# A hybrid retention and attention block: values made token-major, and the last 16 tokens on their own in float32

## The chip, the cores and the metric

The kernel runs on one core of a Trainium2 chip. The core has five engines that run side by side, each with its own queue of instructions: PE (TensorE, matrix multiplies), DVE (VectorE), ACT (ScalarE), POOL (GpSimd) and SP (SyncE, here only the weights' transfers). PE writes its results into PSUM, a small memory of eight banks a partition; everything else lies in SBUF or in the chip's DRAM. The metric is the device time of one execution in microseconds, lower is better.

## The reference

One transformer block, in float32, over 512 tokens with 16 learned "meta" tokens put ahead of them (528 in all), width 1024: a half-weight SwiGLU feed-forward, a mixer, and a second feed-forward. The change touches the mixer.

```python
def hybrid_mixer(u, pos, k_top, w_in, w_ret_out, w_att_out, w_mix_out):
    proj = u @ w_in                       # u: 528 x 1024, normalised
    rq, rk, rv, rg, aq, ak, av, iq, ik, iw, g_ret, g_att = jnp.split(proj, offs, axis=-1)
    rq, rk = rope(rq), rope(rk) * RET_DK ** -0.5          # 4 heads, 256 wide
    yr = retention(rq, rk, rv)                            # values: 4 heads, 512 wide
    yr = (jax.nn.silu(rg) * yr) @ w_ret_out
    ya = dsa_attention(rope(aq), rope(ak), av, rope(iq), rope(ik), iw, k_top) @ w_att_out   # 8 heads, 128 wide
    return (jax.nn.sigmoid(g_ret) * yr + jax.nn.sigmoid(g_att) * ya) @ w_mix_out
```

`retention` weighs the values of each head with decaying scores of query and key. `dsa_attention` picks for each query its 128 best keys by an index score and does a softmax over those and the meta tokens. Both need, for each head, a sum over the tokens of score times value.

## The kernel before, in words

**Layout.** Activations lie feature-major: 128 features on the partitions, the 528 tokens along the free axis; the normalised input is eight such tiles (`xs(0)` to `xs(7)`, KD = 8). Every operand of PE is split into a high and a low part (`split`: ACT copies to the rounded type float32r, DVE subtracts), and a product is three matmuls: high x high, low x high, high x low (`mm3`, L145). A weight tile of 128 columns is loaded by SP's queue (`load_w`; `raw`, two buffers of 1 MB), split (`split_w`, three buffers) and used for 8 x 3 matmuls. Over all 528 tokens a matmul is cut into two of 264 columns (`proj_all`, `halves`), over the 512 tokens whose outputs are kept it has 512 (`proj_real`).

**Order.** The order on PE is that of the code, written out by hand (`manual_schedule`). The other engines' order comes from a planner that goes by priority, program order and the buffers that are free. PSUM in the mixer is two tiles of two banks (`mm_tile`) and four of one bank (`sm_tile`). A buffer is given out again when the last reader of its tile is done.

**Index part** (L568 to 604): four blocks of index queries into the four one-bank tiles (`psiq`), then index keys (`psik`) into the next that comes free; rotary embedding (`rope_swap`) on ACT, POOL and DVE. The scores themselves (`index_steps`) and the selection of keys (`select_steps`) are generators, of which `step()` runs a bit between pieces of other work. The index scores' matmuls (L620) have 64 rows and go in pairs onto the two halves of the array's rows.

**Retention heads** (L803 to 877), for each of four heads: two blocks of queries, two of keys, the output projection of the head before (`last_out`), then for each of four blocks of 128 value columns: the values (`values`, L854: projection into `psrv` over 528 tokens, times the norm R on DVE), the gate (`gated`), and `by_token` (L788): five transposes on PE (L791, L792) that turn the 128 x 528 block into token-major pieces, split into `vh`, `vl` and a small tail tile for the last 16 tokens. `weigh` (L777) then multiplies them with the scores: 12 matmuls and one for the tail (L775), whose three 16-row parts stand at rows 0, 32 and 64 of `vtail`.

**Attention heads** (L974 to 992), for each of eight heads: scores, query and key projections of the next head, transposes of the probabilities (`transpose_p`), the value projection of the next head (`proj_v`, `psav`), the weighing, and `by_token`. In the last head four gates (`gate`, `psgate`) stand where the next head's projections would be; the two other gates of this kind and the eight of the other (`psga`) come after, in the pool `ou`.

Of the kernel before, what the change touches and what calls it, by code (L numbers as in the profile page):

```python
# [81 lines left out]
def kernel(ctx: ExitStack, tc: tile.TileContext, x, meta, g1, wg1, wu1, wd1, gm,  # L82
# [117 lines left out]
    def rstd_steps(ssum, n, dim, dst, sp, psum):  # L200


        ends = [min(b * P, n - P) for b in range(-(-n // P))]
        nb = len(ends)
        col = psum()
        for b, t0 in enumerate(ends):
            nc.tensor.matmul(col[:, b : b + 1], ssum[:, t0 : t0 + P], ones, start=True, stop=True)
        yield from rstd_of(col, n, dim, dst, sp, psum, P - (n - S))

    def rstd_of(col, n, dim, dst, sp, psum, tail):  # L210
# [4 lines left out]
        r = sp.tile([P, 5], F32, tag="rcol", name="rcol", bufs=2)  # L215
# [34 lines left out]
    hd = dpool.tile([KD, P, S], F32, name="hd")  # L250

# [4 lines left out]
    gap(cpool, 8)  # L256


    with pool("f1") as fp, pool("gps", 2, PSUM) as gps, ExitStack() as later:
# [205 lines left out]
        for f0, nf in ((0, 12), (12, 10)):  # L465
# [38 lines left out]
            for c in range(0, KD, 2):  # L504
# [7 lines left out]
                for i in range(2):  # L512
                    k = c + i
                    nc.vector.scalar_tensor_tensor(hT[k], halves(pss[i])[1], 0.5, hT[k], ALU.mult, ALU.add)
                    if f0:
                        h, l = new_x(k, XO)
                        split_gain(hT[k], gains[:, 1, k : k + 1], h, l)
                        add_square(hT[k], ssum2, k == 0, fp, bufs=4)
                        nc.scalar.dma_start(hd[k], hT[k][:, REAL])
# [48 lines left out]
    with pool("ixt") as ixt:  # L568
        tp.update(pool=ixt, bufs=8)
        norm = rstd_steps(ssum2, T, D, R2, ixt, lambda: mm_tile("psn"))  # L570
        pss = []
        cols = Cols(w_in, OFF_IQ, 4)
        for i in range(4):
            w = cols.next()
            ps = sm_tile("psiq")[:, :NL]
            mm3([(ps, LATE)], w, xs, KD)
            pss.append(ps)
            if i < 3:
                next(norm)
        cos, sin = rope_tables(0, ixt)  # L580
# [8 lines left out]
        ps = sm_tile("psik")  # L589
# [60 lines left out]
    def tails(p, n):  # L650

        tp.update(v=[stacked(p, f"vtail{i}", P) for i in range(2)], p=stacked(p, "ptail", n), turn=0)
# [27 lines left out]
    with pool("rt") as rt:  # L680
        tp.update(pool=rt, bufs=7)
        cos, sin = rope_tables(2, rt)
# [85 lines left out]
        def weighted(ps, vb, prob):  # L768

            for kb in range(4):  # L770
                vh, vl = vb[0][:, kb, :], vb[1][:, kb, :]
# [3 lines left out]
            nc.tensor.matmul(ps[:, KQ[4] :], vb[2][:TR], tp["p"][:TR, :NM], start=False, stop=True)  # L775

        def weigh(c, vb, sg, prob, ssum, o):  # L777
# [5 lines left out]
            oh = rt.tile([P, S], F32R, tag=f"oh{c}", name="oh")  # L783
            ol = rt.tile([P, S], F32R, tag=f"ol{c}", name="ol")
            split(t[:, :S], oh, ol)
            o.append((oh, ol))

        def by_token(vt, vp):  # L788
            ps = mm_tile("psvt").rearrange("p (a b) -> p a b", a=2)
            for kb in range(4):  # L790
                nc.tensor.transpose(ps[:, 0, kb * P : (kb + 1) * P], vt[:, kb * P : (kb + 1) * P], ident)  # L791
            nc.tensor.transpose(ps[:NM, 1, 0:P], vt[:, 4 * P : T], ident)  # L792
            vh = vp.tile([P, 4, P], F32R, tag="vh", name="vh", bufs=2)
            vl = vp.tile([P, 4, P], F32R, tag="vl", name="vl", bufs=2)
            split(ps[:, 0, :].rearrange("p (b c) -> p b c", b=4), vh, vl)
            tail = tp["v"][tp["turn"]]
            tp["turn"] ^= 1
            split_rows(ps[:NM, 1, 0:P], tail, "hhl")
            return vh, vl, tail
# [3 lines left out]
        for h in range(RH + 1):  # L803
            if h == RH:
# [4 lines left out]
                break  # L809
            u = rt.tile([P, UW], F32, tag="u", name="u")  # L810
            nc.scalar.dma_start(u, decay[h])
            cols = Cols(w_in, OFF_RQ + h * DK, 2)
            if h == 0:
                steps, bg[0] = bg[0], iter(())
# [9 lines left out]
            cols = Cols(w_in, OFF_RK + h * DK, 2)  # L824
            if h == 0:
                bg[0] = steps
            ka = proj_all(cols, "psrk")
            next(norm, None)
            step()
            kb_ = proj_all(cols, "psrk")  # L830
            next(norm, None)
            rk = rope_pair(ka, kb_, cos, sin, T, "rk")
            step()
# [8 lines left out]
            cv = Cols(w_in, OFF_RV + h * DV, 4)  # L842
# [11 lines left out]
            def values():  # L854
                ps = proj_all(cv, "psrv")
                vt = tmp()
                ins = nc.vector.tensor_tensor(vt, ps, R, ALU.mult)
                step(ins)
                return vt

            for c in range(4):
                if c == 0:
                    sg = gated()
                    vt = values()
                    prob = decayed(rq, rk, u)
                else:
                    vt = values()
                    sg = gated()
                    weigh(*pend, prob, ssum, o)
                if h == 0:  # L870
                    step()
                    step()
                pend = (c, by_token(vt, rt), sg)
# [9 lines left out]

    with pool("ao") as ao:
        ao_parts = []
        with pool("at") as at:
# [11 lines left out]
            cq, ck, cv = (Cols(w_in, o_, AH, step=1) for o_ in (OFF_AQ, OFF_AK, OFF_AV))  # L898
# [20 lines left out]
            def proj_v():  # L919
                w = cv.next()  # L920
                parts, ps = halves(mm_tile("psav"))
                mm3(parts, w, xs, KD)
                vt = tmp()
                nc.vector.tensor_tensor(vt, ps, R, ALU.mult)
                return vt
# [40 lines left out]
            def weigh_v(parts, v):  # L966
                ps = sm_tile("psao")
                weighted(ps, v, parts)
                oh = ao.tile([P, S], F32R, tag=f"ah{len(ao_parts)}", name="ah")
                ol = ao.tile([P, S], F32R, tag=f"al{len(ao_parts)}", name="al")  # L970
                split(ps, oh, ol)
                ao_parts.append((oh, ol))

            q, k, vt = proj_q(), proj_k(), proj_v()  # L974
            for h in range(AH):
                more = h + 1 < AH
                scores(q, k)
                if h == 0:
                    v = by_token(vt, at)
                if more:  # L980
                    q, k = proj_q(), proj_k()
                else:
                    for c in (2, 3, 4):
                        gate_acc(c, gate(gr, at, wide=True))
                parts = transpose_p()
                if more:
                    vt = proj_v()
                else:
                    gate_acc(5, gate(gr, at, wide=True))
                weigh_v(parts, v)  # L990
                if more:
                    v = by_token(vt, at)
# [5 lines left out]
        with pool("ou") as ou:  # L998
            tp.update(pool=ou, bufs=3)
            for c in (6, 7):  # L1000
                gate_acc(c, gate(gr, ou))
            cols = Cols(w_in, OFF_GA, KD)
            sa = []
            for c in range(KD):
                w = cols.next()
                ps = sm_tile("psga")
                mm3([(ps, REAL)], w, xs, KD)
                t = ou.tile([P, S], F32, tag=f"sa{c}", name="sa")
                nc.vector.tensor_tensor(t, ps, Rr, ALU.mult)
                nc.scalar.activation(t, t, AF.Sigmoid)  # L1010
                sa.append(t)
# [54 lines left out]
    mgs.close()  # L1066
    accs.close()
# [117 lines left out]
```

## Time and profile before

| | |
|---|---|
| runs before, us | 1591.03, 1591.54, 1591.64 (median 1591.54) |
| profiled execution | 1590.52 us, span 1588.7 us |
| granted TensorE clock | 0.999 |
| PE busy | 1576.4 us, 99% of the span |
| DVE, ACT, POOL busy | 820.0, 569.3, 230.9 us |
| retention heads, about | 422 to 868 us of the span |
| attention heads, about | 868 to 1076 us |

Rows name line, engine, operation, output<-inputs, shape, count, busy time and mean duration. PE's matmuls overlap: one with 512 columns is shown as 389 ns long, but the next starts 227 ns after it. So starts and stretches are read for PE, not durations. In the timeline and the chain the first two numbers of a row are start and length in us.

### The profile page before, as it was taken

The page shows a single profiled execution, that of the slowest core. Times are in us where ns is not written, and L with a number is a line of the kernel's source. Part 1 is how long each engine was busy: PE and PEld are TensorE (multiplying, and loading weights), DVE is VectorE, ACT ScalarE, POOL GpSimd, SP SyncE. Part 2 cuts the span into 40 slices and gives each one's busy share as a digit, 9 for nine tenths or more (in the row PEclk, how much of TensorE's full clock was granted, in tenths as well). Part 3 has the DMA queues.
Part 4 walks back from the last instruction along what each step waited for, and adds up shares of the span by engine and source line. Part 5 has one row for each costly group of instructions (what it writes and reads, how often), then busy time and mean ns, then how long its engine had stood idle before and what let it go on. Part 6 is the DMA issues. An engine that isn't in the chain of part 4 may idle for free.

```text
span 1588.7 us, 23011 instructions
## 1 busy us (share of the span) xinstructions
PE 1576.4 (99%) x9731; PEld 1419.7 (89%) x9731; DVE 820.0 (52%) x1263; ACT 569.3 (36%) x912; POOL 230.9 (15%) x187
## 2 busy tenths in 40 slices
PE   9999999999999999999999999999999999999998
PEld 8999999999888898899898999988888888888886
DVE  5443234334575776866845766753454444334434
ACT  6322222223544333233333555552234332223223
POOL 1211001111310201302204110011002111001100
PEclk9999999999999999999999999999999999999999
DMA  5222232224422231231313322322233332232222
GB/s 192 83 89 78 97 109 80 97 80 141 134 88 67 67 116 54 80 117 40 120 54 92 95 67 67 93 72 88 91 128 108 111 105 81 94 113 86 93 92 81
DMA packets 148582, 148.66 MB, mean 94 GB/s; under 512 B 3288, under 2 KB 137456, under 8 KB 148480
## 3 DMA queue, kind: packets, MB, share of 16 engines
q1 hardware_dynamic: 143872, 138.16, 27.0%
q10 hardware_dynamic: 4544, 9.03, 1.7%
q8 instruction: 76, 1.25, 0.3%
q14 instruction: 26, 0.21, 0.0%
q0 software_dynamic: 64, 0.01, 0.0%
HBM read 143.00 MB, written 4.19 MB: 93 GB/s over the span
## 4 chain that ended last, share of the span: by engine, by line
PE 94%; DVE 3%; ACT 1%; issue 1%; POOL 1%; DMA 0%; ACTq 0%; POOLq 0%; DVEq 0%
PE psu L152 16%; PE psg L152 15%; PE psd L152 8%; PE psd L1146 7%; PE psrv L152 6%; PE psrg L152 6%; PE psrk L152 3%; PE psak L152 3%; PE psav L152 3%; PE psrq L152 3%; PE psgate L152 3%; PE psro L152 3%; PE psmo L152 3%; PE psaq L152 3%; PE psat L152 3%; PE psga L152 3%
## 5 line engine op out<-in xcount | busy, mean ns | idle before, releaser
L117 ACT ACTIVATE whi<-raw 128x1024 fp32r<-128x1024 f32 (+3 forms) x284 | 278.0, 981 | 840.1 <-PE psu L152 165.5
L118 DVE TENSOR_TENSOR wlo<-raw,whi 128x1024 fp32r<-128x1024 f32 (+3 forms) x284 | 339.7, 1196 | 177.2 <-ACT whi L117 173.6
L152 PE MATMUL psu<-xl,whi 128*128 128x264 f32 (+1 forms) x528 | 141.0, 319 | 0.0
L152 PE MATMUL psu<-xh,whi 128*128 128x264 f32 (+1 forms) x528 | 140.6, 318 | 0.0
L152 PE MATMUL psu<-xh,wlo 128*128 128x264 f32 (+1 forms) x528 | 140.5, 318 | 0.0
L152 PE MATMUL psg<-xl,whi 128*128 128x264 f32 (+1 forms) x496 | 133.3, 321 | 0.0
L152 PE MATMUL psg<-xh,whi 128*128 128x264 f32 (+1 forms) x496 | 132.8, 320 | 0.0
L152 PE MATMUL psg<-xh,wlo 128*128 128x264 f32 (+1 forms) x496 | 132.8, 321 | 0.0
L152 PEld LDWEIGHTS psu<-xh,wlo 128*128 128x128 f32 x528 | 88.1, 188 | 6.8
L152 PEld LDWEIGHTS psu<-xh,whi 128*128 128x128 f32 x528 | 87.8, 188 | 6.9
L152 PEld LDWEIGHTS psu<-xl,whi 128*128 128x128 f32 x528 | 87.5, 188 | 6.9
L152 PEld LDWEIGHTS psg<-xh,wlo 128*128 128x128 f32 x496 | 82.6, 188 | 6.8
L152 PEld LDWEIGHTS psg<-xh,whi 128*128 128x128 f32 x496 | 82.3, 188 | 6.8
L152 PEld LDWEIGHTS psg<-xl,whi 128*128 128x128 f32 x496 | 82.0, 188 | 6.8
L486 POOL TENSOR_TENSOR t<-t,R 128x528 f32<-128x528 f32 x22 | 37.6, 1711 | 262.3 <-ACT t L485 262.3
L1121 POOL TENSOR_TENSOR t<-t,R 128x512 f32<-128x512 f32 x22 | 38.5, 1751 | 251.6 <-ACT t L1120 251.6
L152 PE MATMUL psd<-hl,whi 128*128 128x264 f32 x352 | 71.3, 284 | 0.0
L152 PE MATMUL psd<-hh,wlo 128*128 128x264 f32 x352 | 70.8, 283 | 0.0
L152 PE MATMUL psd<-hh,whi 128*128 128x264 f32 x352 | 70.6, 282 | 0.0
L1146 PE MATMUL psd<-whi,hh 128*128 128x512 f32 x176 | 68.5, 389 | 0.0
L1146 PE MATMUL psd<-wlo,hh 128*128 128x512 f32 x176 | 68.5, 389 | 0.0
L1146 PE MATMUL psd<-whi,hl 128*128 128x512 f32 x176 | 68.5, 389 | 0.0
(316 smaller groups left out, 3543.1 us busy)
## 6 DMA issues: line engine op xcount, KB each, us to landing
raw<-in_w_in_dram SPq DMA_DIRECT2D x34, 1024.0 KB, 4.9
raw<-in_ffn_w_up_dram SPq DMA_DIRECT2D x22, 1024.0 KB, 5.0
raw<-in_ffn_w_gate_dram SPq DMA_DIRECT2D x21, 1024.0 KB, 5.0
raw<-in_w_in_dram SPq DMA_DIRECT2D x25, 512.0 KB, 3.4
raw<-in_ffn_w_down_dram SPq DMA_DIRECT2D x10, 1024.0 KB, 4.8
raw<-in_w_ret_out_dram SPq DMA_DIRECT2D x16, 512.0 KB, 3.4
raw<-in_ffn_w_down_dram SPq DMA_DIRECT2D x8, 768.0 KB, 4.3
raw<-in_ffn_w_down_dram SPq DMA_DIRECT2D x8, 640.0 KB, 3.9
```

Source lines behind the costliest of these rows:

```text
L117: nc.scalar.activation(hi, src, AF.Copy)
L118: eng.tensor_tensor(lo, src, hi.bitcast(F32), ALU.subtract)
L152: nc.tensor.matmul(o, a[:, k, :], b[:, sl], start=first and k == 0 and i == 0, stop=last and k == nk - 1 and i == 2)
L486: nc.gpsimd.tensor_tensor(t, t, R, ALU.mult)
L1121: nc.gpsimd.tensor_tensor(t, t, R, ALU.mult)
L1146: nc.tensor.matmul(pss[b], a[:, bs], m[:, k % 2, :], start=k0 + k == 0 and i == 0, stop=k0 + k == nf - 1 and i == 2)
```

## The change

1. **Values token-major.** `values` takes a head's 512 value columns at once (for attention: four heads at once, twice). The token blocks are now the stationary operand and 512 columns of weights the moving one, by pairs of row blocks of the weights. Four results (`psv`, 128 tokens x 512 columns each) fill both two-bank tiles. They come out token-major, so `by_token` and its transposes go. The norm is applied in the split (`split_gain` with a column of `rtok`), into one high and one low tile `vo`; `weigh` later writes its output over the values that it has used.
2. **The last 16 tokens.** Their part is done in float32, unsplit, from the raw weights: `xlast` holds those 16 columns of the normalised input, padded to 32, for each row block, and 32 matmuls a group write the four 128-column blocks into four groups of 32 partitions of one tile (`psvl`). It is done in two stretches of 16, after the first and the third pair of row blocks.
3. **Their parts through DRAM.** The result is split, both parts are written to a DRAM tile `vd`, and three DMAs bring them to rows 0, 32 and 64 of `vtail`, which is now one tile 512 wide. All five are on POOL's queue.
4. **Gates inside the heads.** Where `proj_v` stood in attention heads 0, 1, 2, 4, 5 and 6 there is now one retention gate each; head 3 has the second half of the values there. The last head has three attention gates. Five of those stay in `ou`.
5. **Order.** In head 0 the keys come ahead of the queries, and index steps run from the start. The scores (`decayed`) come behind all values. `psik` and `psao` take two-bank tiles.

```diff
@@ end of feed-forward 1, for each feature block k
+                        nc.gpsimd.tensor_scalar(xlast[:, k, :NM], hT[k][:, S:], gains[:, 1, k : k + 1], None, ALU.mult)
@@ index part
+        nc.gpsimd.tensor_tensor(xlast[:, :, :NM], xlast[:, :, :NM], R[:, S:].unsqueeze(1).to_broadcast([P, KD, NM]), ALU.mult)
-        ps = sm_tile("psik")
+        ps = mm_tile("psik")[:, :S]
@@ new
+    def values(c0, parts, vp, meanwhile=lambda: None):
+        two = [mm_tile("psv") for _ in range(2)]
+        ps = [two[b // 2][:, b % 2 * S : (b % 2 + 1) * S] for b in range(4)]
+        rest = sm_tile("psvl")[:, :P]
+        for k0 in range(0, KD, 2):
+            if k0 % 4 == 0:
+                raw = wpool.tile([P, 2048], F32, tag="raw", name="raw", bufs=2).rearrange("p (k c) -> p k c", k=4)
+                for i in (0, 2):
+                    rows = slice((k0 + i) * P, (k0 + i + 2) * P)
+                    nc.sync.dma_start(raw[:, i : i + 2], w_in[rows, c0 : c0 + 4 * P].rearrange("(k p) c -> p k c", p=P))
+            wh, wl = split_w(raw[:, k0 % 4 : k0 % 4 + 2, :])
+            for b in range(4):
+                bs = slice(b * P, (b + 1) * P)
+                for k in range(2):
+                    xh, xl = xs(k0 + k)
+                    for i, (a, m) in enumerate(((xh, wh), (xl, wh), (xh, wl))):
+                        nc.tensor.matmul(ps[b], a[:, bs], m[:, k, :], start=k0 + k == 0 and i == 0,
+                                         stop=k0 + k == KD - 1 and i == 2)
+                if k0 == KD - 2:
+                    split_gain(ps[b].rearrange("p (c d) -> p c d", c=4), rtok[:, b : b + 1],
+                               parts[0][:, :, bs], parts[1][:, :, bs])
+                if b % 2:
+                    meanwhile()
+            if k0 % 4 == 0:
+                for k in range(k0, k0 + 4):
+                    for c in range(4):
+                        nc.tensor.matmul(rest[32 * c : 32 * c + 32], xlast[:, k, :], raw[:, k % 4, c * P : (c + 1) * P],
+                                         start=k == 0, stop=k == KD - 1)
+                if k0:
+                    rh, rl = (vp.tile([P, P], F32R, tag=f"rest{i}", name="rest") for i in range(2))
+                    split(rest, rh, rl)
+                    for i, part in enumerate((rh, rl)):
+                        nc.gpsimd.dma_start(vd[i], part.bitcast(F32))
+                    for r, i in ((0, 0), (32, 0), (64, 1)):
+                        nc.gpsimd.dma_start(tp["v"][r : r + NM].bitcast(F32).rearrange("q (c d) -> q c d", c=4),
+                                            vd[i].rearrange("(c q) d -> q c d", q=32)[:NM])
+        return [(parts[0][:, c, :], parts[1][:, c, :], tp["v"][:TR, c * P : (c + 1) * P]) for c in range(4)]
@@ retention head
+            if h == 0:
+                rk = rope_pair(*keys(), cos, sin, T, "rk")
             cols = Cols(w_in, OFF_RQ + h * DK, 2)
...
+            vs = values(OFF_RV + h * DV, parts, rt, step)
+            prob = decayed(rq, rk, u)
...
             for c in range(4):
+                sg = gated()
+                if c:
                     weigh(*pend, prob, ssum, o)
...
-                pend = (c, by_token(vt, rt), sg)
+                pend = (c, vs[c], sg)
@@ attention heads
-            q, k, vt = proj_q(), proj_k(), proj_v()
+            q, k = proj_q(), proj_k()
+            vs = half_values(0)
             for h in range(AH):
                 more = h + 1 < AH
                 scores(q, k)
-                if h == 0:
-                    v = by_token(vt, at)
                 if more:
                     q, k = proj_q(), proj_k()
                 else:
-                    for c in (2, 3, 4):
-                        gate_acc(c, gate(gr, at, wide=True))
-                parts = transpose_p()
-                if more:
-                    vt = proj_v()
+                    wide_gate_a()
+                    wide_gate_a()
+                pt = transpose_p()
+                if h == 3:
+                    more_vs = half_values(1)
+                elif more:
+                    wide_gate()
                 else:
-                    gate_acc(5, gate(gr, at, wide=True))
-                weigh_v(parts, v)
-                if more:
-                    v = by_token(vt, at)
+                    wide_gate_a()
+                weigh_v(h, pt, vs[h])
+                if h == 3:
+                    vs += more_vs
```

## The prediction

> **What bounds the kernel now.** I read the page first: the busy shares, then the chain that ended last, by engine.
>
> ```profile
> span 1588.7 us, 23011 instructions
> PE 1576.4 (99%) x9731; PEld 1419.7 (89%) x9731; DVE 820.0 (52%) x1263; ACT 569.3 (36%) x912; POOL 230.9 (15%) x187
> PE 94%; DVE 3%; ACT 1%; issue 1%; POOL 1%; DMA 0%; ACTq 0%; POOLq 0%; DVEq 0%
> ```
>
> TensorE is busy for all but 12 us of the span, so the question is only how much PE time the change takes out, how much it puts in, and whether a new wait opens. Next come the view of waits with PE as the waiting engine (us in total, times, longest) and the table of windows, for the heads (retention head 1, then all of the attention).
>
> ```profile
> PE psik L152 <- DVE tmp L552: 1.2, 1, 1.2
> PE psrg L152 <- DVE wlo L118: 0.9, 2, 0.6
> PE psst L754 <- DVE tmp L758: 0.5, 1, 0.5
> PE psrq L152 <- ACT tmp L623: 0.5, 1, 0.5
> ...
> 540.00:646.00 106.00, 106.00 (x646) 95.27 (x645) 79.00 (x142) 35.04 (x58) 10.14 (x9) 1.00 0.26 84
> 868.00:1076.00 208.00, 207.95 (x1436) 194.59 (x1435) 139.53 (x314) 113.19 (x227) 33.87 (x32) 1.00 0.28 83
> ```
>
> PE waits for almost nothing, and in both stretches it is busy from end to end, while DVE (79 of 106, 140 of 208 us) and ACT have room. So every microsecond of PE work counts in full, and the gates that move into the attention heads are worth nothing by themselves: they are as many matmuls as before, and there are no holes there for them to fill.
>
> **The profiled execution.** It took 1590.52 us, its span 1588.7 and 1.8 around it, which is 1.0 below the median of 1591.54. I make the sum as a difference and add it to the median.
>
> **Removed: the transposes.** The tile view counts them, the timeline shows one set.
>
> ```profile
> L791 PE MATMUL psvt<-ident,tmp x96: 271/273/329, 463.6 to 1047.7; 128*128 128x128 f32 x96
> L792 PE MATMUL psvt<-ident,tmp x24: 272/273/273, 464.1 to 1047.9; 128*16 128x128 f32 x24
> ...
> 590.58 0.17 PE L775 MATMUL pspv<-ptail,vtail 80*128 80x16 f32 x1
> 590.61 0.65 PE L791 MATMUL psvt<-ident,tmp 128*128 128x128 f32 x4
> 591.09 0.27 PE L792 MATMUL psvt<-ident,tmp 128*16 128x128 f32 x1
> 591.12 0.49 PE L152 MATMUL psrv<-xh,whi 128*128 128x264 f32 x2
> ```
>
> Durations on PE overlap, so starts are what counts. From the first transpose to the first matmul behind the set, 590.61 to 591.12, are 0.51 us. There are 24 sets: 24 x 0.51 = -12.2 us. The two DVE and three ACT instructions of a set, and the multiply by R, go too; they lay beside PE and are worth nothing here.
>
> **Changed: the values' own matmuls.** The chain in order of time gives pure streams (start, us, count).
>
> ```profile
> 577.53 5.78 PE psrv L152 x48
> ...
> 590.76 0.50 PE psvt L791 x4
> 591.26 0.11 PE psvt L792
> 591.37 5.77 PE psrv L152 x48
> ...
> 1353.19 65.28 PE psd L1146 x288
> ```
>
> Before, a group of four 128-column blocks takes 4 x 48 matmuls with 264 columns, 4 x 5.77 = 23.08 us. Afterwards it is 4 row blocks x 8 x 3 = 96 matmuls with 512 columns, tokens stationary and weights moving. L1146 has that form: 65.28 / 288 = 0.227 us each, so 21.76 us. The gain is 1.32 us a group; four retention heads and two attention halves make 6 groups: -7.9 us.
>
> **Added: the last 16 tokens in float32.** That is 8 x 4 = 32 matmuls a group, 192 in all, each with 32 stationary columns and 128 moving ones, on one of four column groups of the array. No such matmul is in the trace, so I bound it. First, what is a float32 matmul there? L207 issues five of them for this norm, and the rows show ten loads and ten matmuls.
>
> ```profile
> 400.74 1.19 PEld L207 LDWEIGHTS psn<-ones,ssum 128*128 128x128 f32 x10 [0.20 <-POOL ssum L245]
> 400.75 1.28 PE L207 MATMUL psn<-ones,ssum 128*128 128x1 f32 x10
> ```
>
> So each becomes two records with a weight load each. How long is a record with 128 float32 columns? The nearest row is the float32 transpose above: 0.11 us from one to the next. So 64 records of 0.11 a group. Can those on different column groups overlap? The nearest rows are the index scores, pairs of matmuls on two row halves of the array.
>
> ```profile
> 451.14 0.39 PE L152 MATMUL psrg<-xh,wlo 128*128 128x512 f32 x1
> 451.46 0.50 PE L620 MATMUL pssc<-ikh,iqh 64*128 64x512 f32 x2
> 451.80 0.40 PE L620 MATMUL pssc<-ikl,iqh 64*128 64x512 f32 x2
> 452.03 0.39 PE L620 MATMUL pssc<-ikh,iql 64*128 64x512 f32 x2
> 452.36 0.51 PE L152 MATMUL psrv<-xh,whi 128*128 128x264 f32 x2
> 452.70 0.28 PE L152 MATMUL psrv<-xl,whi 128*128 128x264 f32 x1
> ```
>
> Two matmuls of 512 columns on different halves together take the 0.23 us of one (451.80 to 452.03), and the next on the same half starts only after that. I carry this over to column groups: different groups overlap, one group doesn't overlap itself. But the two records of one float32 matmul are on one group, and they are neighbours in the queue. If starts keep the queue's order, as all rows here do, the second waits for the first (0.11), the next group's first starts with it, and so on: one record's time for each matmul, not a quarter of it. 32 x 0.11 = 3.5 us a group.
>
> Getting into and out of such a stretch costs too. Entering takes 0.32 us (451.14 to 451.46) against the usual 0.227, the first pair 0.34 against 0.23, leaving 0.33 against 0.23, the first two matmuls behind it 0.34 against the 2 x 0.12 of the stream: about 0.4 in all. The code goes into it twice a group (after row blocks 0 and 1, and 4 and 5): 12 x 0.4 = +4.8.
>
> The ends for 192 such matmuls: all four groups side by side, 16 x 0.11 x 6 = 10.6; no overlap, 64 x 0.11 x 6 = 42.2. The middle is 21.1, and I take it, because the row pairs have this very behaviour. With the switching: +25.9 us.
>
> The Trainium skill (TensorE: Matmul & The Clock Gate, Part 3, Measured speedup vs the span model) counts tiles of the array as starting about 4 ns apart, so that four cost little more than one. By that alone the stretch would have the lower end's 10.6. For row halves the trace agrees (a pair inside one matmul's time), for column groups no run here shows it yet.
>
> **Moved: the keys ahead of the queries in head 0, and psik into a two-bank tile.** There are two such tiles. psik takes the one that the second key projection needs next.
>
> ```profile
> 414.81 0.33 PE L152 MATMUL psiq<-xl,whi 128*128 128x384 f32 x1
> 414.98 0.34 PE L152 MATMUL psiq<-xh,wlo 128*128 128x384 f32 x1
> 416.54 0.47 PE L152 MATMUL psik<-xh,whi 128*128 128x512 f32 x1 [1.22 <-DVE tmp L552]
> ...
> 426.56 1.22 DVE L118 TENSOR_TENSOR wlo<-raw,whi 128x1024 fp32r<-128x1024 f32 x1
> ...
> L592 ACT ACTIVATE tmp<-psik x1: 591/591/591, 428.2 to 428.2; 32x512 f32<-32x512 f32 x1
> L593 ACT ACTIVATE tmp<-psik x1: 590/590/590, 428.8 to 428.8; 32x512 f32<-32x512 f32 x1
> L594 DVE TENSOR_TENSOR tmp<-psik,cos x1: 682/682/682, 429.4 to 429.4; 64x512 f32<-64x512 f32 x1
> L596 DVE TENSOR_TENSOR iw<-psik,R x1: 684/684/684, 430.1 to 430.1; 8x512 f32<-8x512 f32 x1
> ```
>
> psik no longer waits for a bank (416.54 instead of one step of 0.17 after 414.98: -1.4). It then ends near 420.6 (24 x 0.227), the first key block 5.77 later, at 426.4. The second needs psik read out, and the last reader ends at 430.8 behind the ropes of the index queries; the next weights are split only at 427.8. So a new wait of 1.4 to 4.4 us opens; since the readers stand behind the same ropes as before, I take +3.0. Behind the waiting matmul stand the queries of head 0, whose readers wait along. The one multiply of xlast by R on POOL ahead of the tables is inside these bounds.
>
> **Added: the way through DRAM.** Five DMAs a group on POOL's queue: two out, three back. Rows for such transfers, with us to landing, and one issue on POOL:
>
> ```profile
> hd<-hT ACTq DMA_DIRECT2D x8, 256.0 KB, 2.1
> hc<-hd ACTq DMA_DIRECT2D x8, 256.0 KB, 2.6
> grow<-in_mix_norm_dram POOLq DMA_DIRECT2D x1, 4.0 KB, 4.8
> ...
> L277 POOL DMA_DIRECT2D grow<-in_mix_norm_dram x1 | 0.7, 748 | 0.0
> ```
>
> Splits 0.6, two issues 1.4, landing 2.1 to 4.8, one more issue 0.7, landing 2.6 to 4.8: 7.4 to 12.3 us. In the retention heads the reader (L775) comes after the last quarter of the values, the scores and two gates, some 20 us later, and POOL's adds and ropes behind the DMAs aren't due earlier: nothing. The cover is gone in one place. In attention head 3 the second half's values come ahead of weigh_v, and its last matmul reads the same tail tile, which that half has just asked to have rewritten. Its cover is 24 x 0.227 = 5.4 and the 12 matmuls of the weighing, about 2.0. So PE waits 0 to 4.9 us there; I take +2.0, nearer to the rows that go through a DRAM tile. Loads on SP are as many bytes in somewhat more issues, and the other three waits of PE stay: 0.
>
> **The sum.** -12.2 - 7.9 + 25.9 - 1.4 + 3.0 + 2.0 = +9.4 us: 1591.5 + 9.4 = 1601 us.
>
> **Rivals.**
> A: all four column groups run side by side, or a record is half as long (the float32 row that I used is a transpose). Then 10.6 instead of 21.1: -1.1, 1590; with the two new waits at their lower ends (1.4 and 0) -4.7, 1587, which is faster. For it speaks that a pair of row halves costs no more than one matmul, against it the order of the two records. It decides for faster from about 8 us less than my sum up to that end. Chance 0.32. (The rule of the Trainium skill named above would give this case.)
> B: column groups don't overlap at all. +21.1 more: 1622. Against it speak the pairs of row halves; for it, that no row shows columns. Chance 0.15.
> C: DVE becomes the bound, with values' splits and the selection in one stretch. Against it: 79 of 106 us in head 1, and DVE loses work. It would add a few us at most; 0.03, inside the range.
>
> **How the numbers follow.** The forecast's case has 0.5, with its own range of 1594 to 1607 (the waits at their ends, the switching between 0 and its price). Case A reaches from 1585 to 1592, B stands at 1622. A range from 1585 to 1611 leaves out B and a little. Within 0.2% is 1588.4 to 1594.7, about what a measurement can tell. Of A some 0.22 is faster, 0.1 inside; of the forecast 0.03 inside. So faster 0.22, same 0.13, slower 0.65.
>
> **What would show it.** L791 and L792 gone; psv at 0.227 us a matmul; the stretch of 16 float32 matmuls (32 records) about 1.8 us long between its neighbours, against 0.9 in A and 3.5 in B; PE waiting at the second psrk of head 0, and at L775 of attention head 3. Wrong would make me above all the length of that stretch.

## The result, and the profile after

The changed kernel took 1614.42 us (median of 4 runs, 1613.54 to 1616.76) where the kernel before, on the same chip, took 1591.59 (1591.03 to 1591.93): a ratio of 1.0146, 95% interval 1.0129 to 1.0164. It is 22.8 us slower. The forecast was 1601, slower by 9.4, in a range up to 1611: the sign was right, the size was not, and the time lies outside the range. The sign is luck: it comes from a wait that the forecast did not have, and without that wait the terms measured below come out about even. The profiled execution of the changed kernel is its 1613.54 run, with a span of 1611.8 us at a granted clock of 0.998; beside the 1588.7 of before that is 23.1 us, and the sums below are made against these 23.1.

First the page, the span and the busy times, the chain by engine, and one group of instructions:

```profile
span 1611.8 us, 22507 instructions
PE 1575.1 (98%) x9419; PEld 1385.3 (86%) x9419; DVE 803.5 (50%) x1221; ACT 574.9 (36%) x882; POOL 254.5 (16%) x224
...
PE 91%; DVE 3%; ACT 2%; issue 1%; DMA 1%; POOL 1%; ACTq 0%; POOLq 0%; DVEq 0%
...
L683 PE MATMUL psv<-whi,xh 128*128 128x512 f32 x192 | 78.2, 407 | 20.2 <-DVE vo L122 18.9
```

TensorE is busy for 1.3 us less than before, in a span that is 23 us longer. So the loss is not work that PE was given; PE waits. The last row already says where: the matmuls of the values (psv) stood idle for 20.2 us, 18.9 of them until DVE had written vo, the values' low part. The view of waits, PE as the waiting engine (us in total, times, longest), gives the list:

```profile
PE psv L683 <- DVE vo L122: 18.9, 12, 1.7
PE psrk L152 <- DVE iw L605: 3.4, 1, 3.4
...
PE psrq L152 <- ACT wt L619: 1.4, 1, 1.4
PE psv L683 <- DVE tmp L560: 1.3, 1, 1.3
PE psS L980 <- DVE vo L122: 1.0, 1, 1.0
```

Twelve waits of one kind: two in each of the six groups of values. The chain of the changed kernel, in order of time, shows a group's two (start, us, what):

```profile
587.12 1.01 PE psvl L693 x32
588.13 1.60 PE psv L683 x6
...
589.75 0.70 ACT vo L121
...
590.47 0.76 DVE vo L122
...
591.28 3.05 PE psv L683 x12
...
594.35 0.70 ACT vo L121
...
595.07 0.76 DVE vo L122
...
595.88 1.66 PE psv L683 x6
```

The timeline of PE, of the same kernel, around the first of them (start, us, operation, and in brackets the idle time ahead and what ended it):

```profile
586.73 0.39 PE L683 MATMUL psv<-wlo,xh 128*128 128x512 f32 x1
587.05 1.08 PE L693 MATMUL psvl<-raw,xlast 128*32 128x128 f32 x32
588.06 0.50 PE L683 MATMUL psv<-whi,xh 128*128 128x512 f32 x1
588.40 0.40 PE L683 MATMUL psv<-whi,xl 128*128 128x512 f32 x1
...
589.33 0.39 PE L683 MATMUL psv<-wlo,xh 128*128 128x512 f32 x1
591.28 0.50 PE L683 MATMUL psv<-whi,xh 128*128 128x512 f32 x1 [1.56 <-DVE vo L122]
591.61 0.40 PE L683 MATMUL psv<-whi,xl 128*128 128x512 f32 x1
```

This is the last pair of row blocks of a group. Six matmuls finish token block 0; ACT splits off its high part (0.70), DVE its low part (0.76); and only then do the matmuls of token block 1 begin, which have nothing to do with block 0's values. The chain goes PE, ACT, DVE, PE in turn. It happens for blocks 0 to 1 and 2 to 3, and not for 1 to 2. Blocks 0 and 1 lie in one two-bank tile of PSUM, blocks 2 and 3 in the other (`two[b // 2][:, b % 2 * S : ...]`). That the tile as a whole is what a write waits for is tested below.

The second reading is the stretch of float32 matmuls. The tile view of psvl (duration in ns min/median/max, first and last start, shape) counts its records:

```profile
L693 PEld LDWEIGHTS psvl<-raw,xlast x384: 106/110/110, 457.1 to 1024.3; 128*32 128x32 f32 x192
L693 PE MATMUL psvl<-raw,xlast x384: 272/273/298, 457.1 to 1024.4; 128*32 128x128 f32 x192
```

192 matmuls are 384 records, two each. A stretch of 16 (32 records) begins at 587.05, and the next psv at 588.06: 1.01 us, where the forecast said about 1.8, rival A 0.9, rival B 3.5. With both edges, from the start of the last psv ahead (586.73) to that of the second behind (588.40), it takes 1.67, less two ordinary steps of 0.227: 1.22 us a stretch, 14.6 for twelve.

One thing about the changed kernel is no matter of time. In attention head 3 `half_values(1)` stands ahead of `weigh_v`, and both halves keep the last 16 tokens in the one tile `vtail`. The timelines of POOL and of PE have the last transfer into it ahead of the matmul that reads it:

```profile
1031.93 0.51 POOL L701 DMA_DIRECT2D vtail<-vd  x1 [1.08 <-DMA vd<-rest]
1035.85 0.17 PE L828 MATMUL psao<-ptail,vtail 80*128 80x16 f32 x1
```

So the code weighs the last 16 tokens of head 3 with the values of head 7, in the changed kernel and in e1 to e4, e7 and e11 below. The matmuls and transfers are as many either way. In e8 to e10 the second half comes behind that weighing, and each head reads its own values.

### The profile page after: what moved, and what is told of

Its sections match the earlier page's. It is cut to its first block, busy times and chain, and to the rows that moved or that the text cites. A ratio compares the mean times of both kernels' runs of the same rounds, so it can differ in the third digit from the quotient of the medians.

```text
span 1611.8 us, 22507 instructions
## 1 busy us (share of the span) xinstructions
PE 1575.1 (98%) x9419; PEld 1385.3 (86%) x9419; DVE 803.5 (50%) x1221; ACT 574.9 (36%) x882; POOL 254.5 (16%) x224
## 3 DMA queue, kind: packets, MB, share of 16 engines
q8 instruction: 74, 1.21, 0.3%
## 4 chain that ended last, share of the span: by engine, by line
PE 91%; DVE 3%; ACT 2%; issue 1%; DMA 1%; POOL 1%; ACTq 0%; POOLq 0%; DVEq 0%
PE psu L152 15%; PE psg L152 15%; PE psv L683 8%; PE psd L152 8%; PE psd L1182 7%; PE psrg L152 6%; PE psro L152 4%; PE psgate L152 3%; PE psmo L152 3%; PE psga L152 3%; PE psat L152 3%; PE psaq L152 3%; PE psak L152 3%; PE psrq L152 2%; PE psrk L152 2%; PE pspv L827 2%
## 5 line engine op out<-in xcount | busy, mean ns | idle before, releaser
L683 PE MATMUL psv<-whi,xh 128*128 128x512 f32 x192 | 78.2, 407 | 20.2 <-DVE vo L122 18.9
L152 PE MATMUL psro<-vo,whi 128*128 128x512 f32 x256 | 79.1, 390 | 0.0
L683 PE MATMUL psv<-wlo,xh 128*128 128x512 f32 x192 | 75.0, 391 | 0.6 <-DVE wlo L118 0.6
L683 PE MATMUL psv<-whi,xl 128*128 128x512 f32 x192 | 75.0, 390 | 0.0
```

Of the source, the lines that this page charges most:

```text
L152: nc.tensor.matmul(o, a[:, k, :], b[:, sl], start=first and k == 0 and i == 0, stop=last and k == nk - 1 and i == 2)
L683: nc.tensor.matmul(ps[b], a[:, bs], m[:, k, :], start=k0 + k == 0 and i == 0, stop=k0 + k == KD - 1 and i == 2)
```

## The experiments

Ratios are to the kernel before, run on the same chip each time. The first four stand beside the changed kernel; most later ones build on the first.

**e1_split_late: both splits after both blocks of a tile.** If psv waits because a two-bank tile is one thing to those who write it, the waits go with this; the work stays the same.

```
-                if k0 == KD - 2:
-                    split_gain(ps[b] ..., bs)
                 if b % 2:
+                    if k0 == KD - 2:
+                        for d in (b - 1, b):
+                            split_gain(ps[d] ..., ds)
                     meanwhile()
```

> The splits of a pair of token blocks are issued after both blocks' matmuls. Theory 1 (the wait of PE on DVE in the last quarter of the values, 18.9 us in 12 waits, is there because two results share one two-bank tile: the readers of the first half hold back the writes to the second): the 12 waits go, with the 0.11 us of start-up behind each, about -20 us against the changed kernel, 1594 us. Rival (ACT and DVE are simply behind there, and the wait comes back at the next thing that needs them): -5 us at most, 1609 us or more, with new waits at the scores and gates of about the same sum.

Measured: 1595.58 us, ratio 1.0031 (1.0021 to 1.0041), span 1594.6. The same work in another order takes 17.2 us less span than the changed kernel. In the view of waits psv's for vo are gone, and what stays is small:

```profile
PE psrk L152 <- DVE iw L605: 4.4, 1, 4.4
PE psv L683 <- DVE tmp L560: 2.0, 1, 2.0
...
PE psS L982 <- DVE vo L118: 1.4, 1, 1.4
```

How much were the twelve waits worth? From the starts of PE, a group of a retention head is 3.73 us shorter here than in the changed kernel, in each of the four heads (27.98 against 24.24 in head 1). I take the same for the two groups of the attention, whose other waits differ between the kernels (the second one takes 28.07 in the changed kernel, 3.83 above 24.24): 22.4 for six. That is more than the 18.9 of the view, since idle time is counted from a matmul's end, and its row (0.39) is longer than its step (0.227), and since the first step after a wait is 0.1 longer (591.28 to 591.61). Some of it came back as the last rows above: PE reaches other places sooner than ACT and DVE do.

Some came back as clock. The table of windows (us; busy PE, PEld, DVE, ACT, POOL; granted clock, DMA share, GB/s) gives the four us behind the wait for iw, of e1 and then of the changed kernel:

```profile
431.00:435.00 4.00, 3.88 (x19) 3.91 (x20) 2.87 (x4) 2.32 (x3) 0.62 (x3) 0.57 0.67 201
431.00:435.00 4.00, 4.00 (x36) 4.00 (x35) 2.85 (x4) 2.32 (x3) 0.60 (x3) 1.00 0.73 218
```

In e1 the clock granted there is 0.57, and psrk's matmuls start 0.220 apart instead of 0.120, for 16 of them: 1.6 us, which the view of waits does not show.

**e2_alternate: the splits at once, but blocks in the order 0, 2, 1, 3.** If the tile is the unit, it is enough that the next block lies in the other tile.

```
-            for b in range(4):
+            for n, b in enumerate((0, 2, 1, 3)):
```

> Token blocks in the order 0, 2, 1, 3, so that neighbours lie in different two-bank tiles; each is still split at once. Theory 1 (the tile is what is waited for): a split takes 1.7 us, the block in between 1.4, so 6 waits of about 0.4 us are left: -17 us against the changed kernel, about 1597 us. Rival (ACT and DVE behind): no gain beyond 5 us.

Measured: 1598.31, ratio 1.0054 (1.0037 to 1.0071), 16.1 us below the changed kernel's median. Each split has the 1.36 us of six matmuls to be done in, and needs about 1.5; the view of waits has the difference:

```profile
PE psv L683 <- DVE vo L122: 1.0, 5, 0.2
```

**e11_one_bank: the order of the changed kernel, but four one-bank tiles.** The float32 part takes a two-bank tile in exchange; only the group of head 0 keeps the old tiles, so it is the control.

```
-        two = [mm_tile("psv") for _ in range(2)]
...
+        if c0 == OFF_RV:
...
+        else:
+            ps = [sm_tile("psv") for _ in range(4)]
+            rest = mm_tile("psvl")[:, :P]
```

> As the changed kernel, each block split at once, but in all groups except that of head 0 the four results lie in four one-bank tiles and the last 16 tokens' in a two-bank one. Theory (two results in one tile are kept as one thing, so readers of one hold back writes to the other): the two waits in head 0 stay, 3.2 us, the ten others go, about -17 us against the changed kernel at these places; since the scores use the same one-bank tiles next, up to 1.5 us a group come back there: 1597 to 1606 us. Rival (PE waits because its next matmul needs a result of those splits or DVE's queue, wherever the results lie): all 12 waits stay, 1614 us.

Measured: 1602.17, ratio 1.0075 (1.0058 to 1.0091), inside the 1597 to 1606 expected. The view of waits:

```profile
PE psv L687 <- DVE vo L122: 3.1, 2, 1.6
PE psv L687 <- DVE ptl L118: 2.3, 1, 2.3
...
PE psao L832 <- DMA vtail<-vd: 0.7, 1, 0.7
```

Of twelve waits for vo two are left, those of the control (and with one-bank tiles in more use, there are new ones, 2.3 for a bank out of which the probabilities are still split). The work and its order are the changed kernel's; the tile alone differs. With e1 and e2 this settles it: the wait comes from keeping two banks as one tile. Whether the engines would have to wait without that bookkeeping (write into one bank while the other is read) was not tried by taking the wait away, but e11's blocks are such banks, and they do go on side by side.

**e3_order_before: head 0 in the old order.** psik back in a one-bank tile, queries ahead of keys, index steps as before.

```
-        ps = mm_tile("psik")[:, :S]
+        ps = sm_tile("psik")
...
-                rk = rope_pair(*keys(), cos, sin, T, "rk")
+                steps, bg[0] = bg[0], iter(())
...
+            if h == 0:
+                bg[0] = steps
+            rk = rope_pair(*keys(), cos, sin, T, "rk")
```

> Head 0 as in the kernel before: queries ahead of keys, index steps only after them, psik in a one-bank tile; all else as changed. My prediction's step (the move opens a wait at the second key block, 3.4 us in the trace of the changed kernel, and one of 1.4 us at the queries, and takes away 1.4 us at psik): -3 to -4 us, 1611 us. Rival (the index part is bound by its ropes, and PE waits for them elsewhere): within 1.5 us of the changed kernel.

Measured: 1611.79, ratio 1.0132 (1.0117 to 1.0147). By the ratios that is about 2.2 us less than the changed kernel, below the 3 to 4 expected, and the two intervals overlap; the two spans differ by 3.1. The waits for iw and wt are gone; two others take part of their place:

```profile
PE psv L683 <- DVE vo L122: 18.8, 12, 1.6
...
PE psv L683 <- ACT tmp L632: 1.4, 1, 1.4
PE psik L152 <- DVE tmp L560: 1.2, 1, 1.2
```

The last row is the old psik wait (1.2 before, too), which the change had taken away. The moved keys are a trade of some 2 us, and no part of the large loss.

**e4_group_order: the float32 stretch by column groups, c outside, k inside.** Now the eight records that lie on one column group are neighbours in the queue. If a record can start only beside the next one in the queue, a stretch of 32 becomes 29 steps of 0.11; if PE chooses freely, it stays at 8.

```
-                for k in range(k0, k0 + 4):
-                    for c in range(4):
+                for c in range(4):
+                    for k in range(k0, k0 + 4):
```

> The 16 float32 matmuls of a stretch in another order: all four row blocks of one column group, then the next group. Theory (groups overlap only as far as neighbours in PE's queue are on different groups): 32 records of 0.11 us one after another, 3.5 us a stretch in place of 1.1: 12 x 2.4 = +28 us, 1643 us. Rival (PE takes what is ready on another group from further back in its queue): within 5 us of the changed kernel.

Measured: 1631.27, ratio 1.0255 (1.0239 to 1.027), 17 us above the changed kernel: between the two. The timeline of PE, beside the 1.08 above:

```profile
592.06 2.46 PE L693 MATMUL psvl<-raw,xlast 128*32 128x128 f32 x32
594.45 0.50 PE L683 MATMUL psv<-whi,xh 128*128 128x512 f32 x1
```

The single starts tell it. In the changed kernel the 32 records come in eight waves of four: 6 to 7 ns apart within a wave, 0.109 us from wave to wave, and 0.133 from the first to the second (587.052, .059, .065, .072; then 587.185). Here four come alone, then twelve pairs, then four alone: 20 steps. That is what comes out if a group's record can pass over at most three records that wait. Counted through with three, and with the two records of a matmul next to each other, both orders fit, 8 waves of four and these 20 steps; with two the changed kernel would need 9, with four e4 would need 18. Records do not name their column group, so which record stands in which wave is inferred; that groups run side by side, and that 0.109 a record holds within one, are measured.

The Trainium skill (TensorE: Matmul & The Clock Gate, Part 3, Measured speedup vs the span model) gives about 4 ns from tile to tile. The 6 to 7 ns here are a little more. The Trainium skill (the same page, Part 3, The mechanism) says that matmuls start in strict order without reordering. In strict order, with the two records of a float32 matmul next to each other, the changed kernel's stretch would need 17 steps and this one 29; 8 and 20 were seen, so the measurement speaks against it here, as far as the order of the records is known.

**e5_no_rest: e1 without the last 16 tokens.** The float32 matmuls, their splits and the way through DRAM are left out, so the values of the last 16 tokens are missing from the output. This prices the whole part.

> Splits late as in e1_split_late, and the last 16 tokens left out altogether (no float32 matmuls, no way through DRAM; the tail tile stays zero, so the output lacks their part). From the trace of the changed kernel a stretch costs 1.2 us with its switching, so 12 of them 14.5 us: 1581 us. My prediction's price was 25.9 us: 1570 us.

Measured: 1580.32, ratio 0.9934 (0.9919 to 0.9948), 15.3 us less than e1. The trace's 14.6 fits that; the 25.9 of the forecast does not.

**e6_no_dram: e1 without the five DMAs of a group.** The tail of the values stays zero, so the same tokens are missing; the matmuls and splits stay.

> Splits late, float32 matmuls and their split kept, the five DMAs a group left out (the tail tile stays zero, so the output lacks the last 16 tokens' part). Theory: the way through DRAM is hidden, the trace shows no PE wait at the tail's matmuls: within 1.5 us of e1_split_late, 1594 to 1597 us. My prediction's step (it shows once, 2.0 us in attention head 3): 1593.5 us. Rival (POOL's queue, held up by the DMAs, delays ropes and sums elsewhere): 5 us less or more.

Measured: 1594.41, ratio 1.0023 (1.0014 to 1.0032): 1.2 us below e1, with intervals that overlap. The way through DRAM is hidden, but for a microsecond or so, and whether it costs that much these runs do not settle.

**e7_gates_out: e1 with the six gates behind the attention heads.** The forecast held the gates' place inside the heads to be worth nothing. Here they are the same matmuls, after the heads.

```
-                elif more:
-                    wide_gate()
-                else:
+                elif not more:
...
+            while gr.at < gr.n:
+                gate_acc(KD - gr.n + gr.at, gate(gr, ou))
```

> Splits late, the six retention gates taken out of the attention heads and done after them; as many matmuls. My prediction's step (PE has no holes in the heads, so where the gates stand is worth nothing): within 2 us of e1_split_late, 1594 to 1598 us. Rival (without a projection between the transposes of the probabilities and the weighing, PE waits there for the splits of the transposed probabilities, 2 to 3 us in each of 6 heads): +12 to +18 us, 1610 us.

Measured: 1618.4, ratio 1.0172 (1.0155 to 1.0189), span 1617.4: 22.8 us more span than e1. Its waits of PE:

```profile
PE psao L829 <- ACT pth L117: 7.6, 6, 1.3
...
PE psao L829 <- DVE ptl L118: 4.6, 17, 0.4
```

The timeline of PE in one head of the same kernel, from the last transpose of the probabilities into the weighing, with no gate between them:

```profile
943.68 0.27 PE L1000 MATMUL psPT<-ident,pj 128*16 128x128 f32 x1
945.20 0.51 PE L829 MATMUL psao<-pth,vo 128*128 128x512 f32 x1 [1.25 <-ACT pth L117]
...
947.20 0.45 PE L829 MATMUL psao<-ptl,vo 128*128 128x400 f32 x1 [0.35 <-DVE ptl L118]
...
948.52 0.39 PE L829 MATMUL psao<-ptl,vo 128*128 128x256 f32 x1 [0.20 <-DVE ptl L118]
```

Without a gate the weighing waits for each split of the probabilities. The waits sum to 13.1 us in 27 (7.6, 4.6, 0.5 and 0.4); a restart after each, at 0.26 (the 0.16 by which a row is longer than its step, and 0.1), makes about 7 more. The third part is the clock. The table of windows gives the stretch of these heads, here:

```profile
868.00:1055.00 187.00, 172.05 (x1081) 147.47 (x1080) 104.84 (x231) 85.87 (x164) 34.22 (x36) 0.98 0.26 76
```

The same stretch of e1:

```profile
868.00:1055.00 187.00, 182.72 (x1156) 160.22 (x1156) 107.16 (x233) 98.15 (x172) 39.69 (x39) 1.00 0.29 85
```

A clock of 0.98 in place of 1.00 is at most 3.7 us of 187. The starts show two patches of about 3.4 us, near 967 and 1015, in which the matmuls' steps nearly double: some 3 us. Together that is some 23, and 22.8 was measured. So the gate is the cover of these splits, as the projection of the values was before. That is why moving it in costs nothing, and why it could not be left out.

**e8_all_three: e1 with head 0 in the old order, and the waits of the attention heads moved apart.** Keys ahead of queries at the start, the second half's values behind the scores of head 4, one more gate in the heads, and one buffer instead of two for these gates.

Beside the edits of e1 and e3:

```
-            q, k = proj_q(), proj_k()
+            k, q = proj_k(), proj_q()
...
+                if h == 4:
+                    vs += half_values(1)
...
-                if h == 3:
-                    more_vs = half_values(1)
-                elif more:
+                if gr.at < gr.n:
                     wide_gate()
```

> Splits late, head 0 in the order before, and in the attention two moves: keys ahead of queries at the start, so that the values don't wait for the tile that the keys' rope still reads, and the second half's values behind the scores of head 4 instead of between the transposes and the weighing of head 3 (one more gate moves into head 6). Theory (what is left of the loss in e1_split_late is waits for two-bank tiles: 4.4, 2.0, 1.4, 0.4 and 0.4 us in the view of waits, less 1.4 for psik's old wait): about -7 us, 1588.5 us, just under the kernel before. Rival (these waits are where other engines are behind, and come back elsewhere): no less than 1593 us.

Measured: 1588.48 (10 runs), ratio 0.9986 (0.9977 to 0.9996). It is faster than both kernels, and than the kernel before by 2.3 us with nothing left out, a small gain whose interval just clears 1. Of the 7.9 us of span that it lies below e1, some 1.6 are the patch of low clock behind psrk's wait, which its trace does not have. Waits that stay:

```profile
PE psv L683 <- ACT tmp L632: 1.4, 1, 1.4
PE psik L152 <- DVE tmp L560: 1.0, 1, 1.0
...
PE psS L981 <- DVE vo L122: 0.5, 1, 0.5
```

**e9_one_stretch: e8 with the 32 matmuls of a group in one stretch.** That saves six of the twelve entries, at the price of holding the float32 weights longer.

```
+                raws = [raw] if k0 == 0 else raws + [raw]
-            if k0 % 4 == 0:
-                for k in range(k0, k0 + 4):
+            if k0 == 4:
+                for k in range(KD):
```

> As e8_all_three, with the 32 float32 matmuls of a group in one stretch (after the third pair of row blocks) instead of two of 16. Theory (of a stretch's 1.2 us some 0.34 is switching, paid for each stretch): 6 x 0.34 = -2.0 us against e8_all_three, 1586.5 us. Rival (the weights' buffer is given back later, the next load comes late and PE waits): no gain or a loss.

Measured: 1591.32 (11 runs), ratio 1.0005 (0.9996 to 1.0014), 2.8 us above e8. The entries are saved, but two waits of PE take more:

```profile
PE psS L983 <- DVE vo L122: 3.2, 1, 3.2
PE psst L811 <- DVE tmp L815: 1.5, 3, 0.6
```

The timeline of ACT in this kernel, ahead of the first of them:

```profile
902.73 1.06 ACT L117 ACTIVATE whi<-raw 128x1024 fp32r<-128x1024 f32 x1 [1.41 <-DMA raw<-in_w_in_dram]
903.69 1.25 ACT L121 ACTIVATE vo<-psv,rtok 128x512 fp32r<-128x512 f32 x2
```

The weights' buffer comes free later, so the next load starts later, and the split that waits for it stands in ACT's queue ahead of the values' splits, for which the scores wait.

**e10_gate_first: e9 with the first gate ahead of the scores**, so that DVE has time.

```
-            prob = decayed(rq, rk, u)
...
+                if c == 0:
+                    prob = decayed(rq, rk, u)
```

> As e9_one_stretch, with the first gate of each retention head ahead of the scores, as in the kernel before. Theory (DVE has the splits of the last values and then the scores' decay, and PE waits 0.4 to 0.9 us a head for it; a gate in between covers that): -2 us, 1584.5 us. Rival (the weighing then follows after one gate instead of two and waits for the splits of the decayed scores): as much or more lost there, 1587 us or more.

Measured: 1593.84 (11 runs), ratio 1.0019 (1.001 to 1.0028): a miss. DVE has the splits of the values in that time, and now the gate's own weights are late: psrg waits for wlo four times, 2.0 us in all, and psS still waits 3.5. The waits of psst that the move was made for, 1.5 us in e9, are gone.

## Why the prediction was wrong

Each step as the prediction put it, with what the runs showed:

- **"Removed: the transposes", -12.2.** All are gone, and the gain was sized a little small. The single starts of the trace of before show that the first matmul behind each set also took 0.09 longer than its step (0.21 instead of 0.12, or 0.315 instead of 0.227). I counted only up to that matmul's start. 24 x 0.09 makes it -14.3.
- **"Changed: the values' own matmuls", -7.9.** Right: psv goes at 0.227 a matmul; a group in e1 takes 24.24 us, which is 96 x 0.227 and two stretches of 1.22.
- **"Added: the last 16 tokens in float32", +25.9.** The mechanism failed, at "the second waits for the first ... one record's time for each matmul". Two records a matmul and 0.11 a record held; but the second record of one group does not hold up the first of the next. Measured: 8 waves of 0.109, not 16, so +14.6 with the edges (15.3 by leaving it out, e5). Rival A had this term, 10.6 and 4.8 for the switching make 15.4, though not the time: it said 1587 to 1590. (One of its figures does not follow: by the forecast's own sum the change is faster from 9.4 us less, not 8.) I had taken the row halves as the nearest row; but two matmuls on one half next to each other, which is the case that decides, do not occur there.
- **"A gate inside the heads is worth nothing by itself".** It costs nothing, but not for the reason given ("no holes there for them to fill"): taking proj_v out opens holes, and the gates close them. Without them 22.8 us are lost (e7). I should have named the cover.
- **"psik no longer waits", -1.4, and "a new wait of 1.4 to 4.4 us opens" at psrk, +3.0.** Right: 1.2 is gone, and psrk waits 3.4, for the last reader of psik, the one that I named. What I had only as "readers wait along" was a second wait, of head 0's queries for wt: 1.4.
- **"Added: the way through DRAM", +2.0.** Not seen in the changed kernel: its weighing of attention head 3 has no wait for a transfer. Within the bounds of 0 to 4.9, at the lower end. Two runs show it once each, 0.7 us in e11 and 0.4 in e7. I took the rewriting of the tail tile ahead of its reader for a wait alone; as the result section has it, it also changes what head 3 reads. The landing times were 5.0 and 2.3 us, close to the rows that I used.
- **"The other three waits of PE stay: 0".** This is where the prediction was lost. Of ACT and DVE I said that their work "lay beside PE", and for the values' splits I never asked who writes next into the tile that they read. The split of a token block moved from the end of a group to between two blocks of one tile, and PE stood still for it twelve times: 18.9 us in the view of waits, 22.4 with the restarts.

What makes the 23.1 us of span:

| Term | forecast | measured |
|---|---|---|
| transposes | -12.2 | -14.3 |
| values' matmuls | -7.9 | -7.9 |
| float32 matmuls with edges | +25.9 | +14.6 |
| wait for the splits, 6 x 3.73 | none | +22.4 |
| psik, psrk | +1.6 | +2.2 |
| DRAM | +2.0 | 0 |
| queries of head 0 (wt), start of the attention (tmp L560), scores (psS) | none | +4.4 |
| index scores between matmuls of the values, low part of the weights late once | none | +2.2 |
| waits of before that went, less one that came | none | -0.7 |
| sum | +9.4 | +22.9 |

The small terms are each wait of the view with 0.2 to 0.3 added for the restart, and, for the index scores, the starts of PE around their stretches (14.9 us in all before, and 16.3 in e8, which has the changed kernel's order there and no wait in it). The sum is within 0.2 of the span; two errors, +11.3 too much for float32 and 22.4 missing, half hid each other. Had the float32 term alone been right, the forecast would have been a kernel at 1590, and further off.

The verdict on the idea follows from e8: with the splits where they hold nobody up, the change and the other moves of e8 are worth 2.3 us. Its arithmetic (-14.3 - 7.9 + 14.6 = -7.6) is a gain, of which some two thirds are taken back, by the waits that stay and by the index scores' stretches.

## What to carry to other kernels

When a result is read out earlier than before, look up which tile it lies in and who writes into that tile next: here two banks in one tile cost 22 us, and splitting both blocks after both blocks' matmuls gave 17 of them back. When work is moved out from between a producer and its reader, ask what it covered, and put something of the same length there. And a page on which the busy time of the bounding engine falls while the span grows is read from the view of waits, by count: twelve equal waits are one cause.

## What the runs showed of the hardware that was not expected

Four column groups of TensorE, given float32 matmuls in turn, start 6 to 7 ns apart and stream side by side, 32 records in eight steps of 0.109 us, although each matmul is two records on the same group. The order in the queue still counts: with a group's eight records next to each other the stretch took 2.46 instead of 1.08 us (e4), as if a record could pass over three waiting ones and no more. Going into such a stretch and out of it costs 0.34 us in both lengths that were run (1.21 less 0.87 for eight steps; in e9 2.08 less 1.74 for sixteen).

A wait of PE can cost more than itself. In e1 the granted clock fell to half for 3.4 us behind a wait of 4.4 us. In e11 psv's steps went from 0.227 to 0.427 for some 3 us, behind a wait of 2.3 us; behind the 3.4 us of the changed kernel's profile nothing of the kind is seen. So the length of the wait alone does not decide it, and what does stays open.
